# A weight sum taken from VectorE to an adding DMA one block ahead, and DRAM sums spread over a two-layer encoder kernel

## The chip, the cores and the metric

The kernel runs on one NeuronCore of a Trainium2 chip. Its engines run side by side and wait for each other only through semaphores: PE (TensorE, matmuls), DVE (VectorE), ACT (ScalarE), POOL (GpSimd) and SP, which only issues DMAs here. POOL issues DMAs too, and those that add onto their destination are issued by it alone. The metric is the device time of one execution in microseconds.

## The reference, cut to what matters

Two layers work on 512 tokens of width 1024. The first mixes tokens by retention and neighbourhood attention, the second by a state space scan (below: the state space layer). Each is followed by the same channel mixer, and both channel mixers are what the change touches:

```
def conv_geglu_ffn(hn, w_up, conv_w, conv_b, w_down):
    u = depthwise_conv_centered(hn @ w_up, conv_w, conv_b)
    gate, val = jnp.split(u, 2, axis=-1)
    return (jax.nn.gelu(gate, approximate=True) * val) @ w_down
```

w_up is 1024 x 5632 (2816 gate and 2816 value columns), w_down 2816 x 1024. All is float32, and every large product is made of three float32r matmuls: each operand is split into a high part (a cast, on ACT) and a low part (source minus high, on DVE), and high x high, low x high and high x low are summed in PSUM (`mm3`, L125 to L127).

## The kernel before, in words

**The channel mixer's up-projection.** The 2816 columns of each half are 22 tiles of 128, counted by f. Tiles 0 to 5, 20 and 21 are plain. The other 14 are taken in seven Strassen blocks of two tiles each (f = 6, 8, ... 18; blocks 0 to 6 here). A block multiplies a 2 x 2 arrangement of weight quarters (q11, q12, q21, q22, each 128 x 1024 in SBUF) with sums of token halves in seven products (products 0 to 6) instead of eight. A product is 24 matmuls of 128x256. Its stationary operand is a pair of weight parts in one of four places of a buffer named ring. So a place is filled again once the product four before is through, and splitting runs at most about three products ahead of PE.

**What each product needs**, in the function `weights` of `up_strassen`. All loads go through SP.
- Product 0: load q11 into the first-half buffer, split it.
- Product 1: load q12 and q22; DVE adds q12 + q22 into q12 (L469, wst<-wst,wu); DVE adds q11 + q12 into q0 (L469, gain<-wst); POOL issues a DMA that adds a quarter of w_up from DRAM onto q11 (L484); split q12.
- Product 2: split q0. Product 3: load q21, DVE adds it to q0 (L469, gain<-gain), split q0.
- Product 4: split q11, which by then must hold the sum of the DMA above. Products 5 and 6: split q21 and q22.

The three buffers of q11 and q12 (named wst) rotate from block to block; q0 and q21 sit in two others (gain), q22 in wu.

**Around the products.** PSUM results go to tiles G and V by copies (ACT) and adds (DVE, L469). The tails of a block's two tiles (convolution, GELU, product: L531 to L540) are held back and worked off behind products 3 and 5 of the next block. A DVE subtraction of two quarters of H (L329, H<-H, 128x2816), which belongs to the down-projection that follows, becomes ready inside block 3.

**Chores.** The down-projection is a Strassen product as well, and its weight sums are made in DRAM by 32 DMAs per channel mixer (L293, ts): 16 plain copies, then 16 adds, each of a quarter of a quarter (704 KB). They stand in a list. `E.chore()` pops one, ties it to the matmul that was written last, and issues it on POOL. Calls stand in both mixers, behind plain tiles, and in `up_strassen` behind products 1 and 4. In the state space layer they are the letters c in the strings SLOTS, one string per head group, which give the order in which its steps are written: h and i heads and inter-chunk parts, p pairs, n projections of the next group, o output products.

**What sets the order.** Instructions of one engine run in the order in which a scheduler puts them. Split and load of a product have a priority of 60 over their place in the text, and `E.in_turn` keeps them in the order of the products. Across engines only data waits.

Of the kernel before, what the change touches and what calls it, by code (L numbers as in the profile page):

```python
# [8 lines left out]
F32 = mybir.dt.float32  # L9
# [4 lines left out]
ALU = mybir.AluOpType  # L14
# [3 lines left out]
P = 128  # L18
# [385 lines left out]
UP = (6, 8, 10, 12, 14, 16, 18)  # L404
# [41 lines left out]
def up_strassen(E, pool, w_up, f, X, G, V, held):  # L446

    nc, tc = E.nc, E.tc  # L450
    low, high = slice(0, HW), slice(HW, S)

    nth = UP.index(f)
    if f - 2 not in UP:
        E.held = [[E.wst.tile([P, 1024], F32, name="wst") for _ in range(3)],
                  [E.gain.tile([P, D], F32, name="gain") for _ in range(2)]]
    (st12, st11), (st0, st21) = [E.held[0][(2 * nth + j) % 3] for j in range(2)], E.held[1]

    def load(st, s, h):
        E.load = nc.sync.dma_start(st, w_up[s, f + h])  # L460
        return st

    def parts(st, i):
        hi, lo = E.weight(SKEW if i else 0)
        E.split(hi, lo, st)
        E.last = E.pair + (E.load,)
        return hi, lo

    add = lambda o, x, y: nc.vector.tensor_tensor(o, x, y, op=ALU.add)  # L469
    q = {}  # L470

    def weights(i):
        with tc.high_priority(60), E.in_turn():
            if i == 0:
                q[11] = load(st11, 0, 0)
                return parts(q[11], i)
            if i == 1:
                q[12] = load(st12, 1, 0)
                with E.in_turn(E.load):
                    q[22] = load(pool.tile([P, 1024], F32, name="wu", tag=f"e{nth % 2}"), 1, 1)  # L480
                add(q[12], q[12], q[22])
                q[0] = st0
                add(q[0], q[11], q[12])
                nc.gpsimd.dma_start(q[11], w_up[1, f], accum_op=ALU.add, max_dma_last_dim=4096)  # L484
                return parts(q[12], i)
            if i == 2:
                return parts(q[0], i)
            if i == 3:
                q[21] = load(st21, 0, 1)
                add(q[0], q[0], q[21])  # L490
                return parts(q[0], i)
            return parts(q[{4: 11, 5: 21, 6: 22}[i]], i)

    a = E.mm.tile([P, S], F32, name="mm")
    b, d = (E.px.tile([P, S], F32, name="pu", tag="px") for _ in range(2))
    order = ("A11", a), ("S3", b), ("S2", a), ("A22", b), ("R1", a), ("A12", d), ("S4", a)
    for i, (n, bank) in enumerate(order):
        hi, lo = weights(i)
        more = i in (2, 3, 4, 6)
        r = bank.rearrange("p (j c) -> p j c", j=2)  # L500
        for j in range(2):
            for k in range(4):
                c = slice(j * 512 + k * P, j * 512 + k * P + P)
                E.mm3(r[:, j], hi[:, c], lo[:, c], X[n][0][:, k], X[n][1][:, k], not more and j + k == 0, k == 3, more or j > 0)
        if i in (3, 5):
            o = G[:, :, low if i == 3 else high]
            add(o, r, o)
        elif i == 4:
            t = E.tmp.tile([P, 2, HW], F32, name="w5", tag="tmp")
            nc.scalar.copy(t, r)  # L510
            add(V[:, :, low], t, V[:, :, low])
        else:
            nc.scalar.copy({0: G[:, :, high], 1: V[:, :, low], 2: G[:, :, low], 6: V[:, :, high]}[i], r)
        if i in (1, 4):
            E.chore()
        if i in (3, 5) and held:
            held.pop(0)()


def ffn(E, w_up, cw, w_down, ts, g_post_row, done, w1=None):  # L520
# [3 lines left out]
    with ExitStack() as ctx:  # L524
# [44 lines left out]
        for f in range(2, NF):  # L569
            if f in UP or f - 1 in UP:  # L570
                if f in UP:
                    G, V = (cp.tile([P, 2, S], F32, name=n, tag=t) for n, t in
                            ((("G", "k0"), ("V", "k1")) if UP.index(f) % 2 else (("G", "k2"), ("V", "k3"))))
                    up_strassen(E, hp, w_up, f, X, G, V, held)
                    held.extend(partial(tail, f + j, G[:, j], V[:, j], True) for j in range(2))
                    while held and f + 2 not in UP:
                        held.pop(0)()
                continue
            ps = []
            for s in range(2):  # L580
                behind = w1 and f == 2
                with E.in_turn() if f > UP[0] else nullcontext():
                    st = E.wload(w_up[s, f], E.mid if behind and s == 0 else None)
                    w = E.wunit(None, st=st, behind=E.turned[3][1] if behind else None)
                E.last = E.pair + (E.load,)
                ps.append(E.mm.tile([P, S], F32, name="mm"))
                E.proj_fm(ps[-1], w)
            tail(f, *ps)
            E.chore(1 + (f == 2))
            if f < UP[0]:  # L590
                X = next(make)
            if f == NF - 2:
                big = hp.tile([P, 32, HW], R32, name="big")
                for k in range(0, HK, 4):
                    c = slice(k, min(k + 4, HK))
                    E.split(big[:, c], big[:, HK + k:HK + c.stop], H[:, c, HW:])
# [40 lines left out]
def mixer0(E, w0, w_v, w_fm, tabs, dist_d, logit, gn, bias, w_out, g_post_row, done):  # L637
# [286 lines left out]

SLOTS = (
# [4 lines left out]
)  # L930

# [563 lines left out]
```

## Time and profile before

| | |
|---|---|
| median of 3 runs | 1360.77 us (1360.38 to 1362.2) |
| the profiled execution's own time | 1356.96 us |
| its span, first to last instruction | 1355.2 us |
| PE busy | 1325.2 us (98%) |
| DVE busy | 1124.9 us (83%) |
| ACT busy | 841.6 us (62%) |
| POOL busy | 125.5 us (9%) |
| mean granted TensorE clock | 0.998 |

The profiled execution took 3.8 us less than the median of the runs. In the rows below, the columns of the view of stretches are the stretch, its length, then for each engine its busy time and (x) instructions, then the granted clock of PE, the share of the DMA engines and GB/s. A row of the timeline is start, duration, engine, line, operation, out<-in and shape; in brackets, the idle time of the engine before it and what ended that. Matmuls overlap in their records, so PE counts as busy when they follow each other at any pace: the pace is read from the starts.

### The profile page before, as it was taken

What the parts mean: (1) busy time and instruction counts of PE and PEld (TensorE: products, weight loads), DVE (VectorE), ACT (ScalarE), POOL (GpSimd) and SP (SyncE); (2) the same over time, 40 slices, a digit from 0 to 9 for tenths busy, and PEclk for the clock granted to TensorE, in tenths of its full rate; (3) what the DMA queues carried; (4) which work ended last, traced back from release to release, by engine and by line L of the source; (5) the groups of instructions that cost most, each with busy time, mean ns of one, the idle gap of its engine ahead of it and who ended that gap; (6) DMA issues with size and microseconds to landing.
All of it is one profiled execution on the core that took longest, in us unless ns stands there. A gap on an engine that the chain in (4) does not pass through costs nothing.

```text
span 1355.2 us, 20474 instructions
## 1 busy us (share of the span) xinstructions
PE 1325.2 (98%) x7784; PEld 1139.2 (84%) x7784; DVE 1124.9 (83%) x1554; ACT 841.6 (62%) x1353; POOL 125.5 (9%) x144
## 2 busy tenths in 40 slices
PE   7999999999999999999999999999999999999998
PEld 6877777898999988888778788787879899998886
DVE  7368888696799998797878876798789789999886
ACT  5356667453565766664878878477545467666663
POOL 1011111101110000020000110011011111110001
PEclk9999999999999999999999999999999999999999
DMA  8454447348983545564466475285544789684654
GB/s 294 146 208 161 159 135 217 103 123 197 217 206 100 151 143 194 190 210 129 138 181 195 126 247 185 90 250 162 183 133 152 203 197 220 166 225 146 193 183 148
DMA packets 71393, 237.28 MB, mean 175 GB/s; under 512 B 8576, under 2 KB 9344, under 8 KB 70784
## 3 DMA queue, kind: packets, MB, share of 16 engines
q1 hardware_dynamic: 54224, 167.30, 36.8%
q0 software_dynamic: 9184, 53.48, 17.6%
q10 hardware_dynamic: 7888, 15.21, 4.2%
q8 instruction: 61, 1.00, 0.3%
q14 instruction: 36, 0.29, 0.1%
HBM read 228.35 MB, written 51.64 MB: 207 GB/s over the span
## 4 chain that ended last, share of the span: by engine, by line
PE 77%; DVE 10%; ACT 5%; DMA 4%; issue 3%; SPq 1%; POOL 0%; DVEq 0%; POOLq 0%; ACTq 0%
PE mm L125 20%; PE mm L127 20%; PE mm L126 20%; DVE ring L116 3%; PE pu L126 2%; PE pu L125 2%; PE pu L127 2%; DMA pb<-pd 1%; PE pi L1155 1%; PE st L1104 1%; ACT pb L1134 1%; PE py L1175 1%; DVE cv L533 1%; DMA wst<-in_c_fm 1%; PE pt L182 1%
## 5 line engine op out<-in xcount | busy, mean ns | idle before, releaser
L125 PE MATMUL mm<-xh,ring 128*128 128x512 f32 (+1 forms) x880 | 321.0, 365 | 1.3 <-ACT z L1074 0.9
L116 DVE TENSOR_TENSOR ring<-wst,ring 128x1024 fp32r<-128x1024 f32 (+1 forms) x218 | 265.4, 1222 | 67.4 <-ACT ring L115 67.2
L127 PE MATMUL mm<-xl,ring 128*128 128x512 f32 (+2 forms) x880 | 320.0, 364 | 1.1 <-DVE mean L958 0.6
L126 PE MATMUL mm<-xh,ring 128*128 128x512 f32 (+2 forms) x880 | 319.8, 364 | 1.1 <-DVE ring L116 1.1
L115 ACT CAST ring<-wst 128x1024 fp32r<-128x1024 f32 (+1 forms) x218 | 224.4, 1034 | 122.3 <-PE mm L126 64.0
L125 PEld LDWEIGHTS mm<-xh,ring 128*128 128x128 f32 x880 | 165.4, 188 | 29.3 <-issue 2.7
L127 PEld LDWEIGHTS mm<-xl,ring 128*128 128x128 f32 (+1 forms) x880 | 165.1, 188 | 28.1 <-issue 1.1
L126 PEld LDWEIGHTS mm<-xh,ring 128*128 128x128 f32 (+1 forms) x880 | 165.4, 188 | 27.0 <-DVE ring L116 1.7
L125 PE MATMUL mm<-xc,ring 128*128 128x256 f32 x336 | 93.1, 277 | 0.0
L127 PE MATMUL mm<-xc,ring 128*128 128x256 f32 x336 | 93.1, 277 | 0.0
L126 PE MATMUL mm<-xc,ring 128*128 128x256 f32 x336 | 93.1, 277 | 0.0
L1134 ACT ACTIVATE pb<-pb,tok 128x128 f32<-128x128 f32 x256 | 80.7, 394 | 10.0 <-DMA pb<-pd 8.9
L125 PE MATMUL mm<-ring,big 128*128 128x512 f32 x164 | 64.0, 390 | 0.0
L127 PE MATMUL mm<-ring,big 128*128 128x512 f32 x164 | 63.8, 389 | 0.0
L126 PE MATMUL mm<-ring,big 128*128 128x512 f32 x164 | 63.8, 389 | 0.0
L127 PEld LDWEIGHTS mm<-xc,ring 128*128 128x128 f32 x336 | 63.1, 188 | 0.0
L125 PEld LDWEIGHTS mm<-xc,ring 128*128 128x128 f32 x336 | 63.1, 188 | 0.0
L126 PEld LDWEIGHTS mm<-xc,ring 128*128 128x128 f32 x336 | 63.0, 188 | 0.0
L125 PE MATMUL pu<-xh,ring 128*128 128x256 f32 x224 | 62.5, 279 | 0.1
L126 PE MATMUL pu<-xh,ring 128*128 128x256 f32 x224 | 62.3, 278 | 0.1
L127 PE MATMUL pu<-xl,ring 128*128 128x256 f32 x224 | 62.1, 277 | 0.0
L293 POOL DMA_DIRECT2D ts<-in_f_down x48 | 31.0, 652 | 280.3 <-PE mm L127 229.5
(360 smaller groups left out, 3120.8 us busy)
## 6 DMA issues: line engine op xcount, KB each, us to landing
ts<-in_f_down POOLq DMA_DIRECT2D x48, 704.0 KB, 6.3
wst<-in_f_up SPq DMA_DIRECT2D x60, 512.0 KB
wst<-in_c_fm SPq DMA_DIRECT2D x40, 512.0 KB
wst<-ts SPq DMA_DIRECT2D x32, 512.0 KB
pb<-pd ACTq DMA_DIRECT2D x29, 512.0 KB
wst<-in_f_down SPq DMA_DIRECT2D x24, 512.0 KB
ts<-ts POOLq DMA_DIRECT2D x16, 704.0 KB, 7.2
wst<-in_ab_fm SPq DMA_DIRECT2D x20, 512.0 KB
```

The costliest lines, as they stand in the source:

```text
L115: first = self.nc.scalar.copy(hi, src)
L116: second = self.nc.vector.tensor_tensor(lo, src, hi.bitcast(F32), op=ALU.subtract)
L125: mm(out, lh, rh, start=first, stop=False)
L126: mm(out, ll, rh, start=False, stop=False)
L127: self.product = mm(out, lh, rl, start=False, stop=last)
L182: last = nc.tensor.transpose(pt[:, j], xs[:, j * P:(j + 1) * P], self.ident)
L293: out.append(lambda i=i, src=src, j=j, c=c, kw=kw: gp.dma_start(part(ts, i, c), part(src, j, c), **kw))
L533: nc.vector.scalar_tensor_tensor(o[:, :S - 1], ps[:, 1:], w(2), o[:, :S - 1], op0=ALU.mult, op1=ALU.add)
L1104: nc.tensor.matmul(ps, o["bt"][:, c], xs, start=True, stop=True)
L1134: nc.scalar.activation(pb[:, dr, c], pb[:, dr, c], AF.Identity, scale=1.0 - 2 * dr, bias=tok[:, 0, c, dr * H + h:dr * H + h + 1])
L1155: nc.tensor.matmul(pi[:, c - 1 + dr], o["st"][dr, i][:, q * P:(q + 1) * P], o["t"][1][:, c * C:(c + 1) * C], start=True, stop=True)
L1175: E.together([nc.tensor.matmul(py[j * 64:j * 64 + 64, c * C:(c + 1) * C], o["x"][:, c, (2 * q + j) * 64:(2 * q + j + 1) * 64], ms[j][0][:, c],
```

## The change

Of the sums that a block needs, q12 + q22 is no longer made by DVE, except in block 0. In each block but the last, SP loads the next block's q12 into the third of the rotating buffers (`ahead`), and POOL issues a DMA that adds the next block's q22 from DRAM onto it (`onto`). The block's own q22 is still loaded into wu for product 6; that load now stands behind the load of q21. Each load is kept behind the one before it. `E.chore()` behind product 1 goes, so a block issues one chore and not two. Four letters c are added in the strings of head groups 1 and 2 of the state space layer: four chores of the second channel mixer, plain copies, are issued there instead of later.

```diff
--- before.py
+++ after.py
@@ -454,11 +454,19 @@
     if f - 2 not in UP:
         E.held = [[E.wst.tile([P, 1024], F32, name="wst") for _ in range(3)],
                   [E.gain.tile([P, D], F32, name="gain") for _ in range(2)]]
-    (st12, st11), (st0, st21) = [E.held[0][(2 * nth + j) % 3] for j in range(2)], E.held[1]
-
-    def load(st, s, h):
-        E.load = nc.sync.dma_start(st, w_up[s, f + h])
+    first, more_blocks = f - 2 not in UP, f + 2 in UP
+    (st12, st11, ahead), (st0, st21) = [E.held[0][(2 * nth + j) % 3] for j in range(3)], E.held[1]
+
+    def load(st, s, h, f=f):
+        with E.in_turn(E.load):
+            E.load = nc.sync.dma_start(st, w_up[s, f + h])
         return st
+
+    def onto(st, f, h):
+        nc.gpsimd.dma_start(st, w_up[1, f + h], accum_op=ALU.add, max_dma_last_dim=4096)
+
+    def load22():
+        q[22] = load(pool.tile([P, 1024], F32, name="wu", tag=f"e{nth % 2}"), 1, 1)
 
     def parts(st, i):
         hi, lo = E.weight(SKEW if i else 0)
@@ -475,18 +483,24 @@
                 q[11] = load(st11, 0, 0)
                 return parts(q[11], i)
             if i == 1:
-                q[12] = load(st12, 1, 0)
-                with E.in_turn(E.load):
-                    q[22] = load(pool.tile([P, 1024], F32, name="wu", tag=f"e{nth % 2}"), 1, 1)
-                add(q[12], q[12], q[22])
+                q[12] = st12
+                if first:
+                    load(st12, 1, 0)
+                    load22()
+                    add(st12, st12, q[22])
                 q[0] = st0
                 add(q[0], q[11], q[12])
-                nc.gpsimd.dma_start(q[11], w_up[1, f], accum_op=ALU.add, max_dma_last_dim=4096)
+                onto(q[11], f, 0)
                 return parts(q[12], i)
             if i == 2:
+                if more_blocks:
+                    load(ahead, 1, 0, f + 2)
+                    onto(ahead, f + 2, 1)
                 return parts(q[0], i)
             if i == 3:
                 q[21] = load(st21, 0, 1)
+                if not first:
+                    load22()
                 add(q[0], q[0], q[21])
                 return parts(q[0], i)
             return parts(q[{4: 11, 5: 21, 6: 22}[i]], i)
@@ -511,7 +525,7 @@
             add(V[:, :, low], t, V[:, :, low])
         else:
             nc.scalar.copy({0: G[:, :, high], 1: V[:, :, low], 2: G[:, :, low], 6: V[:, :, high]}[i], r)
-        if i in (1, 4):
+        if i == 4:
             E.chore()
         if i in (3, 5) and held:
             held.pop(0)()
@@ -924,8 +938,8 @@
 
 SLOTS = (
     "G s0 s1 t6 t7 s2 i0 h0 t8 t9 S h1 p0 i1 n0 h2 h4 h3 p1 i2 n6 n1 h5 n7 i3 n9 p2 N n3 n4 n2 n5 h6 h7 p3 n8 N",
-    "s0 G R s1 s2 h0 i0 i1 o0 c h1 h2 o1 c p0 h4 h3 p1 h5 i2 n0 c n1 p2 n6 c n3 h6 n7 n2 n9 N i3 n8 h7 p3 n4 n5 N",
-    "G R s0 s1 o0 c h2 o1 c s2 h0 h1 i1 i0 p0 h3 p1 h4 i2 n0 c h5 N n1 n3 c p2 n2 n4 i3 h6 h7 p3 n5 N",
+    "s0 G R s1 s2 h0 i0 i1 o0 c h1 h2 o1 c p0 h4 h3 p1 h5 i2 n0 c n1 p2 n6 c n3 h6 n7 n2 c n9 N i3 n8 c h7 p3 n4 n5 N",
+    "G R s0 s1 o0 c h2 o1 c s2 h0 h1 i1 i0 p0 h3 p1 h4 i2 n0 c h5 N n1 n3 c p2 n2 c n4 c i3 h6 h7 p3 n5 N",
     "G R h0 s0 s1 c t9 h1 t8 c s2 i0 t6 S h2 c t7 p0 i1 S h3 o0 c p1 i2 h4 h5 o1 p2 i3 h6 h7 p3",
 )
 
```

The lines of the changed kernel stand 8 to 14 lower behind this place: L469 is L477 there, L484 is L466, and L532, L533 and L540 are L546, L547 and L554. On PE the order of all matmuls is the same.

DVE in the second channel mixer, from the split for product 6 of block 3 to the split for product 1 of block 4 (ring<-wu: split for product 6; the ring<-wst after it: product 0; the next ring<-wst: product 1; cv: tails). Before:

```order
L116 TENSOR_TENSOR ring<-wu,ring 128x1024
L469 TENSOR_TENSOR G<-pu,G 128x2x256
L329 TENSOR_TENSOR H<-H 128x11x256
L469 TENSOR_TENSOR V<-w_10722,V 128x2x256
L116 TENSOR_TENSOR ring<-wst,ring 128x1024
L469 TENSOR_TENSOR wst<-wst,wu 128x1024
L469 TENSOR_TENSOR G<-pu,G 128x2x256
L532 SCALAR_TENSOR_TENSOR cv_10753<-G,cwt,cv_10753 128x511
L469 TENSOR_TENSOR gain<-wst 128x1024
L533 SCALAR_TENSOR_TENSOR cv_10753<-G,cwt,cv_10753 128x511
L116 TENSOR_TENSOR ring<-wst,ring 128x1024
```

And in the changed kernel:

```order
L329 TENSOR_TENSOR H<-H 128x11x256
L477 TENSOR_TENSOR G<-pu,G 128x2x256
L116 TENSOR_TENSOR ring<-wu,ring 128x1024
L116 TENSOR_TENSOR ring<-wst,ring 128x1024
L477 TENSOR_TENSOR V<-w_10724,V 128x2x256
L477 TENSOR_TENSOR gain<-wst 128x1024
L477 TENSOR_TENSOR G<-pu,G 128x2x256
L116 TENSOR_TENSOR ring<-wst,ring 128x1024
L546 SCALAR_TENSOR_TENSOR cv_10755<-G,cwt,cv_10755 128x511
L546 SCALAR_TENSOR_TENSOR cv_10760<-V,cwn,cv_10760 128x511
L547 SCALAR_TENSOR_TENSOR cv_10755<-G,cwt,cv_10755 128x511
L547 SCALAR_TENSOR_TENSOR cv_10760<-V,cwn,cv_10760 128x511
L116 TENSOR_TENSOR ring<-gain,ring 128x1024
```

The add wst<-wst,wu is gone, H<-H stands ahead of the split for product 6 and no longer behind it, and two convolution steps moved from ahead of the split for product 1 to behind it.

POOL in the second channel mixer, blocks 1 to 4 (wst with the same number is the same buffer). Before, where each wst row is the sum for product 4 of one block:

```order
L484 DMA wst_9899<-in_f1_up 128x1024
L293 DMA ts1_221<-in_f1_down 176x1024 x2
L484 DMA wst_9901<-in_f1_up 128x1024
L293 DMA ts1_221<-in_f1_down 176x1024
L293 DMA ts1_221<-ts1_221 176x1024
L484 DMA wst_9900<-in_f1_up 128x1024
L293 DMA ts1_221<-ts1_221 176x1024 x2
L484 DMA wst_9899<-in_f1_up 128x1024
```

And in the changed kernel, where of each two wst rows the first is the sum for product 4 of a block, and the second, once that buffer is read and loaded again, the q12 + q22 of the block two further on:

```order
L466 DMA wst_9903<-in_f1_up 128x1024 x2
L293 DMA ts1_221<-ts1_221 176x1024
L466 DMA wst_9905<-in_f1_up 128x1024 x2
L293 DMA ts1_221<-ts1_221 176x1024
L466 DMA wst_9904<-in_f1_up 128x1024 x2
L293 DMA ts1_221<-ts1_221 176x1024
L466 DMA wst_9903<-in_f1_up 128x1024 x2
```

Three DMAs a block stand there as before, one more of them an add onto SBUF and one fewer a chore, and each sum for product 4 now has a chore and an add of a whole quarter just ahead of it.

## The prediction

> **What bounds the kernel now.** I read the page's first part, then the waits of PE, then the stretches of the Strassen blocks, and last the timeline of DVE and ACT where PE waits.
>
> ```profile
> span 1355.2 us, 20474 instructions
> PE 1325.2 (98%) x7784; PEld 1139.2 (84%) x7784; DVE 1124.9 (83%) x1554; ACT 841.6 (62%) x1353; POOL 125.5 (9%) x144
> ...
> PE pt L182 <- DVE xs L173: 9.9, 4, 7.3
> PE pu L126 <- DVE ring L116: 4.2, 2, 2.2
> ```
>
> PE is the bound, and its order of matmuls doesn't change. So the change can only win what PE loses around the Strassen blocks. The second wait is there: PE waits for a low part of a split, twice, 4.2 us. What it costs is seen in the stretches of one block each (first channel mixer blocks 3 to 6, second blocks 0 to 6 without 3):
>
> ```profile
> 398.21:417.84 19.63, 19.57 (x170) 19.37 (x169) 19.49 (x21) 12.10 (x17) 0.28 (x1) 1.00 0.52 146
> 417.84:442.30 24.46, 22.10 (x170) 21.55 (x169) 23.15 (x28) 15.20 (x20) 0.87 (x1) 0.93 0.37 109
> 442.30:462.20 19.90, 19.90 (x170) 19.90 (x169) 19.90 (x24) 13.59 (x18) 0.86 (x1) 1.00 0.51 159
> 462.20:481.74 19.54, 19.54 (x170) 19.54 (x169) 19.54 (x25) 14.88 (x20) 0.89 (x1) 1.00 0.53 162
> ...
> 1083.42:1102.62 19.20, 19.20 (x169) 19.18 (x168) 14.36 (x15) 10.90 (x13) 3.52 (x4) 1.00 0.82 180
> 1102.62:1121.83 19.21, 19.21 (x171) 19.21 (x169) 16.79 (x20) 13.78 (x18) 2.68 (x3) 1.00 0.88 210
> 1121.83:1141.03 19.20, 19.20 (x171) 19.20 (x169) 19.03 (x23) 13.06 (x17) 2.68 (x3) 1.00 0.90 215
> ...
> 1160.22:1182.68 22.46, 20.37 (x170) 19.97 (x169) 22.46 (x27) 15.28 (x20) 2.68 (x3) 1.00 0.73 187
> 1182.68:1202.59 19.91, 19.89 (x171) 19.70 (x170) 19.91 (x24) 13.59 (x18) 2.68 (x3) 1.00 0.90 227
> 1202.59:1221.81 19.22, 19.22 (x171) 19.22 (x169) 19.22 (x25) 14.56 (x20) 1.82 (x2) 1.00 0.72 184
> ```
>
> An undisturbed block takes 19.2 us, 2.72 a product and 2.88 for product 0. DVE's share of it grows from 14.36 to all of it (22.46 of 22.46). Above 19.2 the first mixer pays 0.43 + 5.26 + 0.70 + 0.34 = 6.7 us, the second 3.26 + 0.71 + 0.02 = 4.0. **10.7 us is the most that can be won here.** Block 4 holds most of it:
>
> ```profile
> 421.40:423.60 2.20, 0.01 (x1) 0.00 (x0) 2.20 (x4) 2.17 (x4) 0.87 (x1) 1.00 0.00 0
> 424.50:427.90 3.40, 3.40 (x18) 3.40 (x17) 3.40 (x5) 0.00 (x0) 0.00 (x0) 0.50 0.96 235
> 1163.30:1165.40 2.10, 0.08 (x2) 0.00 (x1) 2.10 (x4) 2.07 (x4) 0.89 (x1) 1.00 0.00 0
> ```
>
> PE stands for 2.20 and some 2.1 us, and in the first mixer the granted clock then is 0.50 for 3.40 us: 1.7 us more. The rest is pace: block 5 takes 0.7 us more with next to no wait, because matmuls that were once held up follow each other more slowly for a while. (The Trainium skill, "TensorE: Matmul & The Clock Gate", section "What's actually happening", lets the clock fall to half after an idle window of about 3.4 us. The trace differs: 2.20 us were enough once. By the rule 1.7 of the 10.7 us would not be there to win; by the row they are.)
>
> **Why PE waits**, second mixer, end of block 3 and start of block 4 (DVE, and one row of ACT):
>
> ```profile
> 1155.20 3.08 DVE L329 TENSOR_TENSOR H<-H 128x2816 f32<-128x2816 f32 x1
> 1158.20 0.69 DVE L469 TENSOR_TENSOR V<-w,V 128x512 f32<-128x512 f32 x1
> 1158.80 1.22 DVE L116 TENSOR_TENSOR ring<-wst,ring 128x1024 fp32r<-128x1024 f32 x1
> 1159.93 1.22 DVE L469 TENSOR_TENSOR wst<-wst,wu 128x1024 f32<-128x1024 f32 x1
> 1161.07 0.68 DVE L469 TENSOR_TENSOR G<-pu,G 128x512 f32<-128x512 f32 x1
> 1161.67 0.74 DVE L532 SCALAR_TENSOR_TENSOR cv<-G,cwt,cv 128x511 f32<-128x511 f32 x1
> 1162.33 1.22 DVE L469 TENSOR_TENSOR gain<-wst 128x1024 f32<-128x1024 f32 x1
> ...
> 1164.13 1.22 DVE L116 TENSOR_TENSOR ring<-wst,ring 128x1024 fp32r<-128x1024 f32 x1
> ...
> 1161.24 1.05 ACT L115 CAST ring<-wst 128x1024 fp32r<-128x1024 f32 x1 [4.25 <-DVE wst L469]
> ```
>
> DVE never rests. From start to start a 128x1024 operation costs 1.13 us, a 512-wide one 0.60, a convolution step 0.66, H<-H 3.00. The cast for product 1 itself waits 4.25 us for the add that the change removes. A full block asks of DVE ten 1024-wide operations, three 512-wide adds and two tails of four steps and a product: 11.3 + 1.8 + 6.5 = 19.6 us against PE's 19.2. That is why the lead melts, and the 3.00 us of H<-H finish it.
>
> **The change, part by part.** *The add by DVE.* It goes in six blocks of seven, in both mixers:
>
> ```profile
> L469 DVE TENSOR_TENSOR wst<-wst,wu 128x1024 f32<-128x1024 f32 x14 | 17.1, 1219 | 0.0
> ```
>
> 12 x 1.13 = 13.6 us of DVE. A block then asks 18.5 us, under PE's 19.2, so the lead no longer melts from block to block. To see whether H<-H still hits PE, I run down DVE's new order in the prices above. The lead is the time from the end of a low part to its product. At product 0 of block 3 I take the 5.65 us that block 2's has (low part 1114.95 + 1.23, product at 1121.83), the ring being full:
>
> ```profile
> 1109.25 1.23 DVE L116 TENSOR_TENSOR ring<-wst,ring 128x1024 fp32r<-128x1024 f32 x1 [1.48 <-ACT ring L115]
> ...
> 1114.95 1.23 DVE L116 TENSOR_TENSOR ring<-wst,ring 128x1024 fp32r<-128x1024 f32 x1 [0.40 <-ACT ring L115]
> ...
> 1121.83 0.28 PE L125 MATMUL mm<-xh,ring 128*128 128x256 f32 x1
> ```
>
> Up to product 1 of block 4, DVE has 2.9 + 3.7 + 4.2 + 1.8 + 2.5 + 5.3 + 1.1 + 3.5 = 25.0 us to do, PE eight products, 22.1: a lead of 2.8. Before, it was 1160.22 + 2.88 - (1164.13 + 1.22) = -2.2. The same count over the old order, from block 2's product 0, has 48.2 us of work against 41.3 of PE and gives -1.2, so it flatters by 0.5 a block. Two products on, 3.8 and 4.2 us of work face 5.4 of PE: 0.2. From this 0.5 comes off for that error, and up to 0.9 because product 4's split may wait for its DMA. So product 3 of block 4 is late by 0.3 to 1.2 us. Then PE again pays some 0.7 us in pace, as block 5 shows. I leave 1.0 to 2.8 us per mixer, centre 1.8, and the 0.50 clock is not met, since it came behind 2.20 us of standing and not behind 2.1.
>
> Sum: 10.7 - 2 x 1.8 = **7.1 us saved**; bounds 10.7 (nothing left) and 5.1 (2.8 left in each).
>
> *The DMAs on POOL.* Twelve more adds of 512 KB from DRAM onto SBUF; the trace has 14 of this kind:
>
> ```profile
> L484 POOL DMA_DIRECT2D wst<-in_f_up x14: 860/888/908, 331.2 to 1203.5; - x14
> ...
> DMA to landing us min/median/max: 5.2/7.0/9.6
> ```
>
> A block's q12 sum is issued once product 4's split of the block two back is read and the buffer loaded again, over 20 us ahead of its split. Even 9.6 us hides. Tighter is the sum for product 4, which now has a chore and such an add before it:
>
> ```profile
> 1097.84 0.86 POOL L293 DMA_DIRECT2D ts<-in_f_down  x1 [7.36 <-PE mm L127]
> 1099.98 0.88 POOL L484 DMA_DIRECT2D wst<-in_f_up x1 [1.27 <-DVE V L469]
> 1108.16 1.05 ACT L115 CAST ring<-wst 128x1024 fp32r<-128x1024 f32 x1 [1.44 <-DMA wst<-in_f_up]
> ...
> 1113.66 0.28 PE L125 MATMUL mm<-xc,ring 128*128 128x256 f32 x1
> ```
>
> 2.1 us behind a chore it took 8.2 us, the cast waited for it, and the low part ended 1110.48: 3.2 us of lead at 1113.66. The added DMA goes out about 6 us before it (the split for product 4, 3 us for the load, then POOL) and should be through: cost 0. From both sides: a gain of nothing, since a chore stood there before too; a loss of 3.0 us a DMA still in flight (8.2 - 5.2) would use up the 3.2 us and no more.
>
> At this place a rule speaks against the change. The Trainium skill ("SBUF — State Buffer", section "SBUF: two separate sides", the "DVE blocks DMA" trap) says that descriptors of POOL's DMAs can't be written while DVE holds a port that both share in its two-port modes. The trace disagrees for these operations:
>
> ```profile
> L484 POOL DMA_DIRECT2D wst<-in_f_up x1: 891/891/891, 463.1 to 463.1; - x1
> ...
> DMA to landing us min/median/max: 5.2/5.2/5.2
> ```
>
> At 463.1 DVE is busy all of the stretch (19.54 of 19.54), and the landing is the fastest of all. By the rule the new sums would land only when DVE pauses, which is rival 2 with its 1369 us; by the row they cost nothing and the sum stays 7.1.
>
> *Loads, chores.* SP issues as many loads as before; q22's moves behind q21's but is needed three products later. A second chore per block goes: no engine waited for those. The four copies in the state space layer stand in POOL's queue ahead of `sq` adds:
>
> ```profile
> 808.79 0.53 POOL L293 DMA_DIRECT2D ts<-in_f_down  x1
> 841.68 1.28 POOL L1187 TENSOR_TENSOR sq<-sq 128x512 f32<-128x512 f32 x1 [32.37 <-ACT sq L1181]
> ```
>
> POOL idles 32.37 us there, and the copies wait for matmuls that end before the `sq`. Cost 0; if their traffic holds up weights or rows, about 1 us, hence 0 to 1. The last two chores now fall on tiles 20 and 21, three products of the down-projection before they are read.
>
> **Rivals.**
> 1. *The stall only moves.* H<-H now stands ahead of the split for product 6 of block 3 and still takes 3.00 us. If the lead at block 3 is 3 and not 5.65 us (a late DMA left 3.2), product 6 and products 2 and 3 of block 4 each come late, and half of the 10.7 stays, with one clock drop of 1.7: saved 2 to 4, 1357 to 1359, 1358 in the middle. Against it: 3.4 us less DVE work by then.
> 2. *The sum for product 4 becomes the bound* (slower). If the added DMA and the chore both are in flight before it, it takes 5.2 + 2 x 3.0 to 5.2 + 2 x 4.4 (9.6 - 5.2) = 11.2 to 14.0 us from issue. From 3.2 us of lead at 8.2, it decides from 11.4 on: 0 to 2.6 us in each of blocks 1 to 6. The middle, 1.3 x 12 = 15.6, less 7.1: 8.5 slower, 1369. For it: DMA engines at 0.90 in blocks with three POOL DMAs. Against: those blocks had no late product 4.
> 3. *It doesn't show*: other DVE waits, or the state space layer, take back 5 of 7 us: 1359 to 1363.
>
> **How the numbers follow.** The sum stands against the profiled execution: 1356.96 - 7.1 = 1349.9. That one is 3.8 us under the median of the runs; I leave this difference as it is: 1360.77 - 7.1 = **1353.7 us**, own range 1350 to 1356.5. About 0.2% (2.7 us) is what a measurement can tell from no change, so faster is below 1358.0 and slower above 1363.5. Chances: forecast 0.62, rival 1 0.17, rival 2 0.09, rival 3 0.12. Faster: 0.62, half of rival 1 and a little of rival 3's edge, together 0.73; slower 0.09; same 0.18. Range for 8 in 10: the forecast's own, rival 1 and the start of rival 3: 1349.5 to 1359.5.
>
> **What would show it.** Right: no PE wait of 2 us for ring in either block 4, granted clock at 1.00 through both mixers, blocks 5 at 19.2 to 19.5, DVE with idle time in blocks 1 to 3, and a small wait at product 3 of block 4. Rival 1: a wait at product 6 of block 3, or one over 1.5 us at product 3. Rival 2: casts of wst that wait for DMA wst in every block, landings over 11 us. Wrong altogether: block lengths as before with the add gone, so that DVE's sum was not what held PE; or PE waits in the state space layer at the new copies.

## The result, and the profile after

The changed kernel takes 1378.22 us (median of 4 runs, 1377.01 to 1381.16), the kernel before 1360.58: ratio 1.014, 95% interval 1.0116 to 1.0164, so 1.4% slower. The prediction was 1353.7, in a range from 1349.5 to 1359.5: the wrong side of no change.

The profiled execution took 1377.01 us. The page's first lines, and the longest waits of PE, of the changed kernel:

```profile
span 1375.2 us, 20491 instructions
PE 1331.0 (97%) x7784; PEld 1143.0 (83%) x7784; DVE 1112.4 (81%) x1542; ACT 839.9 (61%) x1353; POOL 134.6 (10%) x156
...
PE pu L125 <- ACT V L527: 16.4, 12, 2.0
PE pt L182 <- DVE xs L173: 9.7, 4, 7.3
PE mm L125 <- DVE xf L1082: 4.7, 3, 3.0
```

DVE did become lighter (1124.9 to 1112.4), and the wait for `ring` of product 1 (4.2 us, two times) is gone. In its place stands a new wait, 12 times: once in each of blocks 1 to 6 of both channel mixers, always ahead of product 3, for ACT's copy V<-pu that empties the PSUM bank of product 1. A third row, 4.7 us for xf, belongs to the state space layer.

The view of stretches by stage shows where the span grew. Before (first mixer's blocks, a stretch of 50 matmuls in the state space layer, second mixer's blocks), then after:

```profile
340.61:481.85 141.24, 138.82 (x1178) 138.06 (x1177) 131.38 (x150) 92.59 (x121) 11.54 (x13) 0.99 0.63 166
848.16:859.42 11.26, 10.45 (x52) 8.48 (x51) 5.96 (x8) 7.90 (x17) 0.00 (x0) 1.00 0.26 87
1083.43:1221.81 138.38, 136.28 (x1178) 135.67 (x1176) 130.82 (x149) 92.55 (x121) 17.87 (x20) 1.00 0.83 202
```

```profile
340.39:488.01 147.62, 138.92 (x1178) 137.52 (x1177) 126.23 (x144) 92.33 (x121) 16.16 (x18) 1.00 0.72 177
854.52:870.02 15.50, 12.31 (x52) 9.52 (x50) 5.95 (x8) 9.84 (x23) 0.00 (x0) 0.89 0.26 101
1093.33:1241.80 148.47, 140.61 (x1178) 139.38 (x1177) 126.37 (x144) 92.28 (x122) 16.99 (x19) 0.99 0.73 177
```

The same matmuls take 6.4 us more in the first mixer and 9.9 in the second (the last stretch ends 0.2 us behind the mark used for that difference), 4.2 in the one short stretch of the state space layer; everything else together is 0.5 shorter, which makes the 20.0 us between the two spans. In the short stretch the granted clock is 0.89: 3.41 us of it run at half clock, so 1.7 of the 4.2 us come from the clock. Between the medians lie 17.6 us; the first profile of the kernel before was an execution 3.6 us under its median.

The new wait, followed back in block 2 of the first mixer, in the timeline of POOL, ACT and PE and the view of DMA landings:

```profile
374.00 0.86 POOL L466 DMA_DIRECT2D wst<-in_f_up  x1 [17.36 <-DMA wst<-in_f_up]
375.50 0.91 POOL L293 DMA_DIRECT2D ts<-ts  x1 [0.64 <-PE mm L127]
376.39 0.95 POOL L466 DMA_DIRECT2D wst<-in_f_up  x1
...
L466 POOL DMA_DIRECT2D wst<-in_f_up x1: 952/952/952, 376.4 to 376.4; - x1
DMA to landing us min/median/max: 11.9/11.9/11.9
...
388.33 1.05 ACT L115 CAST ring<-wst 128x1024 fp32r<-128x1024 f32 x1 [3.33 <-DMA wst<-in_f_up]
389.82 0.57 ACT L527 COPY V<-pu 128x512 f32<-128x512 f32 x1
...
390.44 0.39 PE L125 MATMUL pu<-xh,ring 128*128 128x256 f32 x1 [1.38 <-ACT V L527]
```

Three DMAs go out within 2.4 us: the q12 sum for a later block, the chore, and last the one that is needed first, the sum for product 4. It lands after 11.9 us. ACT's cast for product 4 waits 3.33 us for it, the copy of product 1 is queued behind that cast (with a step of a tail between them), and PE can't start product 3 because its bank isn't empty. In the twelve blocks PE stands 0.8 to 2.1 us longer between two matmuls there than elsewhere, goes on at a slower pace, and once, in block 1 of the second mixer, has half the clock for 3.4 us.

The two blocks 4 carry the same name in that row of waits, but not the same cause. Here is the one of the second mixer, ACT, DVE and PE:

```profile
1184.64 1.05 ACT L115 CAST ring<-gain 128x1024 fp32r<-128x1024 f32 x1 [2.42 <-DVE gain L477]
1185.60 1.04 ACT L115 CAST ring<-wst 128x1024 fp32r<-128x1024 f32 x1
1185.85 1.22 DVE L116 TENSOR_TENSOR ring<-gain,ring 128x1024 fp32r<-128x1024 f32 x1
1187.18 0.39 PE L125 MATMUL pu<-xh,ring 128*128 128x256 f32 x1 [1.07 <-ACT V L527]
```

The cast for product 4 waits for no DMA: its sum took 6.7 us and had landed. ACT waited for DVE, and product 3's own low part ends only at 1185.85 + 1.22 = 1187.07. In the first mixer the cast waits 0.35 us for the sum, and 2.43 for DVE stand ahead of it. These two waits, 2.3 of the 16.4 us, are mostly DVE's; the other ten are the late sum's.

The place in the state space layer, POOL, ACT and PE of the changed kernel, then ACT of the kernel before:

```profile
843.29 0.49 POOL L293 DMA_DIRECT2D ts<-in_f_down  x1 [14.88 <-PE mm L127]
847.28 1.52 ACTq L1137 DMA_DIRECT2D pb<-pd  x1
856.84 2.79 ACT L1148 ACTIVATE pb<-pb,tok 128x128 f32<-128x128 f32 x9 [5.38 <-DMA pb<-pd]
859.54 0.76 ACT L1079 ACTIVATE xf<-mm,cwt 128x512 f32<-128x512 f32 x1
860.82 0.47 PE L125 MATMUL mm<-ring,yh 128*128 128x512 f32 x1 [2.97 <-DVE xf L1082]
```

```profile
840.91 0.37 ACTq L1123 DMA_DIRECT2D pb<-pd  x1
846.26 2.75 ACT L1134 ACTIVATE pb<-pb,tok 128x128 f32<-128x128 f32 x9 [1.18 <-DMA pb<-pd]
```

One of the four added chores goes out 4.0 us ahead of a row load (pb<-pd) and lands 2.6 us behind the start of that load. ACT waits 5.38 us for rows where it waited 1.18, the evacuation of xf stands behind that, and PE waits 2.97 us. It is the same shape as in the mixers: a DMA that is late stops ACT's queue, and a PSUM bank behind it stays full.

### The profile page after: what moved, and what is told of

It reads as the page before. It is cut to its first block, busy times and chain, and to the rows that moved or that the text cites. A ratio compares the mean times of both kernels' runs of the same rounds, so it can differ in the third digit from the quotient of the medians.

```text
span 1375.2 us, 20491 instructions
## 1 busy us (share of the span) xinstructions
PE 1331.0 (97%) x7784; PEld 1143.0 (83%) x7784; DVE 1112.4 (81%) x1542; ACT 839.9 (61%) x1353; POOL 134.6 (10%) x156
## 5 line engine op out<-in xcount | busy, mean ns | idle before, releaser
L1148 ACT ACTIVATE pb<-pb,tok 128x128 f32<-128x128 f32 x256 | 80.8, 392 | 15.7 <-DMA pb<-pd 14.3
L125 PE MATMUL pu<-xh,ring 128*128 128x256 f32 x224 | 64.2, 287 | 16.4 <-ACT V L527 16.4
L115 ACT CAST ring<-gain 128x1024 fp32r<-128x1024 f32 x42 | 44.1, 1049 | 23.9 <-DVE gain L477 21.4
```

Of the source, the lines that this page charges most:

```text
L115: first = self.nc.scalar.copy(hi, src)
L125: mm(out, lh, rh, start=first, stop=False)
L1148: nc.scalar.activation(pb[:, dr, c], pb[:, dr, c], AF.Identity, scale=1.0 - 2 * dr, bias=tok[:, 0, c, dr * H + h:dr * H + h + 1])
```

## The experiments

**Where does PE hang, at the bank or at the split?** Theory A: the order on ACT makes the price, since the copy of product 1 stands behind a cast that waits. Theory B: the sum itself is too late, wherever the copy stands. The edit ties the cast for product 4 behind the copy:

```diff
-        with tc.high_priority(60), E.in_turn():
+        with tc.high_priority(60), E.in_turn(*E.last, *([E.copied] if i == 4 else [])):
```

> The changed kernel, with the copy of product 1 (V<-pu) put ahead of the cast for product 4 in ACT's order, and nothing else. Theory A (the late sum stops ACT's queue: the cast for product 4 waits for the adding DMA, the copy that empties product 1's bank stands behind it, and PE waits for the bank at product 3): the sum still lands 11 to 12 us after its issue, the twelve waits of PE for V<-pu (16.4 us) are gone, since product 4's low part ends 0.4 to 1.2 us ahead of where an undisturbed PE would want it; blocks of 19.2 to 19.8 us, 1353 to 1361 us in all. Theory B (product 4's own split is what holds PE): the waits only move from product 3 to product 4, time within 4 us of 1378.

Measured: 1376.39 us, ratio to before 1.0143 (1.0107 to 1.0178). The copies of product 1 are no longer waited for, but the waits go on (longest waits of PE, then block 3 of the first mixer):

```profile
PE mm L125 <- ACT G L527: 10.8, 9, 2.4
...
L466 POOL DMA_DIRECT2D wst<-in_f_up x1: 1237/1237/1237, 397.7 to 397.7; - x1
DMA to landing us min/median/max: 14.1/14.1/14.1
...
411.82 1.05 ACT L115 CAST ring<-wst 128x1024 fp32r<-128x1024 f32 x1 [3.34 <-DMA wst<-in_f_up]
413.72 0.58 ACT L527 COPY G<-mm 128x512 f32<-128x512 f32 x1
414.34 0.55 PE L125 MATMUL mm<-xc,ring 128*128 128x256 f32 x1 [2.24 <-ACT G L527]
```

PE now waits one product later, at product 4, for the copy of product 2, and the low part of product 4's split ends only 0.2 us earlier. Block 1 of the first mixer, with a landing of 12.2 us, ran without a wait, but in blocks 2 and 3 the sums landed after 13 and 14 us, since PE was no longer held back and all that POOL issues came closer together. Theory B holds in the main. The order on ACT decides at which product the wait shows, and has a part of the price: the mixers are 12.6 us longer than before in e1 and 16.3 in the changed kernel (3.4 and 1.7 of that is half clock).

**Why is the sum late?** Either because of the two DMAs ahead of it in POOL's queue (A1) or for some other reason, such as the traffic of loads (C). One run takes the chore from ahead of it, one the q12 sum, one both.

```diff
-        if i == 4:
+        if i == 1:          # e2; e5: if i == 2
             E.chore()
...
-                    onto(ahead, f + 2, 1)          # e3 and e5:
+                    E.together([onto(ahead, f + 2, 1)], [E.product])
```

> The changed kernel, with the one chore of a block behind product 1 and no longer behind product 4, so that only the next block's q12 sum is in flight just ahead of the sum for product 4. Theory A1 (two DMAs in flight ahead of it make that sum late): it lands 8 to 9 us after issue, the waits at product 3 are gone, 1353 to 1361 us. Theory C (the sum is slow for another reason, as the traffic of loads or 26 adding DMAs in place of 14): landing still over 10 us, most of the 16.4 us of waits stay, 1370 or more.

> The changed kernel, with the next block's q12 sum tied to the end of product 1 of the running block, so that only a chore is in flight just ahead of the sum for product 4. Theory A1: it lands 8 to 10 us after issue, as before the change; waits at product 3 gone, q12 sum ready 5 us or more ahead of its cast, 1353 to 1361 us. Theory C: landing over 10 us, 1370 or more.

> The changed kernel with both moves: the next block's q12 sum tied to the end of product 1 of the running block, the chore behind product 2. If POOL's DMAs are worked off one behind the other, the sum for product 4 now meets an empty queue and lands in 5 to 6 us in every block; no PE wait at product 3 or 4 for it; both channel mixers together 7 to 9 us shorter than in the kernel before, the state space layer still some 5 us longer: 1355 to 1358 us. If the sums are slow by something else than their place in the queue: landings above 8 us as in the two single moves, and no gain over those (1358 and 1363.5).

| | time, us | ratio to before (95%) | landing of the sum for product 4, blocks 1 to 6, first mixer | mixers against the first profile of before |
|---|---|---|---|---|
| changed kernel | 1378.22 | 1.014 (1.0116 to 1.0164) | 8.0 to 11.9 | +6.4, +9.9 |
| e2, chore moved | 1357.98 | 0.9992 (0.9972 to 1.0012) | 5.3 to 10.5 | -3.8, -1.6 |
| e3, q12 sum moved | 1363.55 | 1.0027 (1.0009 to 1.0046) | 5.3 to 10.3 | -2.8, +1.3 |
| e5, both moved | 1356.65 | 0.9971 (0.9953 to 0.9988) | 5.5 to 9.2 | -4.2, -1.5 |

As what makes most of the price theory C is out: with the same 26 adding DMAs and the same loads, only their order changed, the two mixers together are 21.9 us shorter in e5 than in the changed kernel (16.3 to -5.7; 1.7 of it is the half clock in block 1). Moving the chore alone already brings 21.6. Not every number came as expected: e2's landings spread wider than 8 to 9 us, and e3's 1363.55 lies above the 1353 to 1361 that were forecast, with a sum of 10.9 us in block 2 of the second mixer (that block 1.4 us longer) and 3.0 us in the state space layer's short stretch.

The order isn't all of it. For block 6 no q12 sum goes ahead, only a chore, 2.3 us ahead and onto an empty queue. Its landing in the changed kernel, first mixer:

```profile
L466 POOL DMA_DIRECT2D wst<-in_f_up x1: 896/896/896, 463.6 to 463.6; - x1
DMA to landing us min/median/max: 10.9/10.9/10.9
```

The chore took 9.4 us there and the sum 10.9 (10.5 in the second mixer), where the kernel before, with a chore 2.1 to 2.3 us ahead, had sums of 8.2 to 8.9; PE waited in both blocks 6. SP issued three loads between 457.5 and 458.4, just ahead of the two; that their traffic made the difference was not tested.

For e5 too my number for the landings was wrong. Here is the landing in block 2 of the first mixer, then in block 4 (view of DMA landings):

```profile
L466 POOL DMA_DIRECT2D wst<-in_f_up x1: 914/914/914, 375.9 to 375.9; - x1
DMA to landing us min/median/max: 8.5/8.5/8.5
...
L466 POOL DMA_DIRECT2D wst<-in_f_up x1: 896/896/896, 418.2 to 418.2; - x1
DMA to landing us min/median/max: 5.7/5.7/5.7
```

I expected 5 to 6 us in every block. The chore, issued 6.4 us ahead, stood itself behind the q12 sum and was still under way. Where the chore was through, as in block 4, the sum took 5.7; in block 6, where it was all but through (it landed 0.4 us later), 8.2. What the sum still costs in e2 and e3 comes with landings around 10 us (block 2 of e2: 10.5, and that block is 1.3 us longer; block 2 of e3: 10.3, 0.7 longer). With those of up to 9.2 us in e5 some casts for product 4 still wait, up to 1.74 us, but PE doesn't. What waits of PE for V<-pu are left in e5 stand in block 4 of both mixers, at product 3:

```profile
427.33 0.38 PE L125 MATMUL pu<-xh,ring 128*128 128x256 f32 x1 [0.73 <-ACT V L527]
1171.40 0.39 PE L125 MATMUL pu<-xh,ring 128*128 128x256 f32 x1 [0.56 <-ACT V L527]
...
426.01 1.21 DVE L116 TENSOR_TENSOR ring<-gain,ring 128x1024 fp32r<-128x1024 f32 x1
```

The first mixer's low part for product 3 is ready only at 426.01 + 1.21 = 427.22: DVE again, at the place and with the size (0.3 to 1.2 us) that the prediction's count gave.

**What is it worth to free DVE?** The kernel before without the add q12 + q22; the sum is left out, so q12 enters its products alone, and no DMA takes its place.

```diff
                 q[12] = load(st12, 1, 0)
...
-                add(q[12], q[12], q[22])
```

> The kernel before without the add q12 + q22: the sum is left out, q12 goes alone into its products, and no DMA takes its place. It measures what freeing DVE is worth by itself. By the prediction's count (18.5 us of DVE work in a block of 19.2): PE's waits in both blocks 4 and the 0.50 clock are gone, 5 to 9 us less, 1352 to 1356 us. If DVE's add is not what held PE: 1359 to 1362.

Measured: 1355.56 us, 0.9957 (0.9943 to 0.9971), 5 us less. Block 4 of both mixers, view of stretches:

```profile
419.12:439.06 19.94, 19.91 (x171) 19.72 (x169) 19.90 (x24) 13.88 (x19) 1.62 (x2) 1.00 0.48 136
1160.42:1180.97 20.55, 19.89 (x170) 19.70 (x169) 20.52 (x25) 14.48 (x19) 3.57 (x4) 1.00 0.84 201
```

Before they took 24.46 and 22.46 (23.06 and 22.42 in another profile of the same kernel, e9 below). So DVE's add was what held PE there.

**What is left of it?** By the prediction the 3.0 us of H<-H. In e6 and e8 both moves are kept, and two of the chores added in the state space layer, those of head group 2, go to product 5 of the last two blocks (`if i == 2 or i == 5 and nth > 4`); e8 also makes H<-H in three pieces:

```diff
-            tt(A21, A11, A21, op=ALU.subtract)
+            for c in (slice(0, 4), slice(4, 8), slice(8, HK)):
+                tt(A21[:, c], A11[:, c], A21[:, c], op=ALU.subtract)
```

> As with both moves, and besides the two chores added in head group 2 of the state space layer go to product 5 of the last two Strassen blocks (the two in head group 1 stay). If these two alone held the row loads up: no PE wait of over 1.5 us for xf there, the layer within 1 us of the kernel before, and 3 to 5 us less than with both moves alone: 1350 to 1354 us. If the two of head group 1 matter as much: half of that, 1353 to 1356.

> As e6 (both moves, two chores moved), and H<-H of 128x2816 split in three pieces of 1024, 1024 and 768, which may stand in blocks where DVE idles. If the 3.0 us of this one operation are what is left in blocks 3 to 5 (3 to 4 us in both mixers after the single move of the chore): blocks 3 to 5 at 19.2 to 19.4, 1 to 3 us less than e6, 1348 to 1352. If what is left comes from the sums or the loads: equal to e6.

e6 takes 1357.27 us (0.9971, 0.9958 to 0.9983), no less than e5 and above both ranges that were expected of it. e8 takes 1353.62 (0.9942, 0.9921 to 0.9964). Block 4 of both mixers in e8:

```profile
417.24:437.05 19.81, 19.81 (x170) 19.80 (x169) 19.77 (x25) 14.68 (x20) 2.68 (x3) 1.00 0.81 206
1158.83:1178.64 19.81, 19.81 (x170) 19.80 (x169) 19.77 (x25) 14.68 (x20) 2.68 (x3) 1.00 0.82 201
```

Against the first profile of before the mixers are 4.4 and 2.3 us shorter in e6, 6.2 and 3.4 in e8: 9.6 of the 10.7 us that were there to win. H<-H was most of what was left: blocks 5 and 6 are at 19.2 us in e8, block 4 keeps 0.6 in each mixer, and at 1353.62 it stays above the expected 1348 to 1352. That e6 gained nothing on e5 spoke against my choice of the guilty chores, which the next runs settle.

**What do the chores in the state space layer cost?** In e4 the kernel before gets the four chores alone: the order on POOL is the only one that differs. e10 is e8 with none of the four (they go to product 5 of the last four blocks), e11 is e8 again beside it, and e9 the kernel before once more, for its profile.

> The kernel before, with the four further chores in the state space layer alone. If these copies by themselves delay the row loads (pb<-pd) for which ACT waits, and with them PE: PE waits of 1.5 and 3 us for xf in head group 2, 3.5 to 5 us more in the layer, 1364 to 1366 us. If the delay in that layer came only from the phase in which the first channel mixer left the kernel: 1360 to 1361 us.

> The kernel before once more, for its profile. The state space layer was 2.8 us longer than in the first profile of the kernel before even in the kernel without the add, whose order of chores there is the old one. If the layer's length changes by some us from execution to execution: this profile has it 1 to 5 us longer than the first too. If the first profile is what this kernel always does there: within 0.5 us of it.

> As e8 (both moves, H<-H in three pieces), with the state space layer's chores as in the kernel before: none of the four is added there, they go to product 5 of the last four Strassen blocks. If the added chores cost 3 to 5 us in that layer: 1349 to 1351. If the layer varies by itself and the chores cost under 1 us: within 1 us of e8's 1353.6.

> The kernel of e8 once more, on the same chip as e10, to compare the two: 1352 to 1355 us.

e4: 1362.71 us, 1.0026 (1.0006 to 1.0046), between its two expected ranges. e9: 1358.49. e10: 1350.95, 0.9929 (0.991 to 0.9948). e11: 1353.23, 0.9951 (0.9933 to 0.9969). The stretch of 50 matmuls shown above, first in e4, then in e8, then in e10:

```profile
850.48:864.64 14.16, 10.68 (x52) 8.40 (x50) 5.93 (x8) 9.78 (x23) 0.00 (x0) 1.00 0.28 105
```

```profile
843.48:858.83 15.35, 10.72 (x51) 8.39 (x50) 5.93 (x8) 9.78 (x23) 0.00 (x0) 1.00 0.26 97
```

```profile
844.24:855.40 11.16, 10.45 (x52) 8.47 (x50) 5.97 (x8) 7.81 (x17) 0.00 (x0) 1.00 0.24 89
```

It is 2.6 to 4.9 us longer in all nine profiles with the added chores of head group 1 (the changed kernel, e1 to e6, e8, e11), and within 0.2 us of the first profile of before in the three that don't (e7, e9, e10). e6 and e8 show that those of head group 2, which I had moved, are not the ones. So two chores of head group 1 cost this stretch some 3 to 5 us; in five of the nine (the changed kernel, e1, e2, e5, e11) 1.7 of it is half clock behind the wait. Not all of it reaches the end. The part of the layer ahead of this stretch is 0.8 us longer in the changed kernel, up to 4.4 in others, and 3.2 in e9, which is the kernel before: it varies from execution to execution. In e6, e7 and e9, the three with more than 3 us, 1.7 of that is again half clock. In the medians of e10 and e11 2.3 us are left.

## Why the prediction was wrong, point by point

- **The sum for product 4** is the step that failed: "should be through: cost 0". I counted on some 6 us between the added DMA and it, and took 3.0 us for each DMA still in flight. Measured: 5.4 us in block 1 of the first mixer, 2.4 to 3.9 in all others that have such a DMA ahead (blocks 1 to 5) but the two blocks 4 (6.9 and 7.6), because the buffer that the added DMA fills is free only once product 4's split is through, and that split was late itself. And the two others in flight cost together up to 6.7 us of 11.9 (11.9 less the 5.2 of a sum alone), in the second mixer up to 7.5 of 12.7. In place of nothing it cost 21.9 us (the mixers of the changed kernel against e5). What made the sums of block 6 late, with only a chore ahead, is open in part.
- **Rival 2** named the mechanism, with a chance of 0.09 and 8.5 us slower; it came out 17.6 slower. Its lead of 3.2 us was read at the low part of product 4, where it decides from 11.4 us of landing on. In the changed kernel ACT's copy of product 1 stands behind the cast, and PE needs the bank a product earlier, so it decided from some 10 us on (10.5 in e2 cost 1.3 us, 9.2 in e5 nothing). I had not asked what is queued behind the waiting cast on ACT, though the prediction quoted that cast with its wait. What stood "against" it didn't carry over: in such a block of the kernel before the three DMAs went out over 11.4 us (1128.00 to 1139.36), here within 2.4 in block 2 of the first mixer, since the late product 4 made the next added DMA late.
- **By DVE's load** the forecast was right. The block's sum of 18.5 us against 19.2, and with it the end of the stall in block 4, came as said: block 4 of the first mixer took 20.96 us in the changed kernel, where the wait at product 3 was mostly DVE's, and 19.9 in e7. The term of 7.1 us, bounded by 5.1 and 10.7, measured 4.7 in e7, 5.7 in e5 and 6.8 in e6. Against e9's profile in place of the first one each of these is 1.1 us less. What e6 leaves over, 2.3 and 1.7 us, lies in the 1.0 to 2.8 a mixer that were left for H<-H, though the 2.8 are more than the parts named there (1.2 of lateness and 0.7 of pace) add up to. e5 shows the wait at product 3 of block 4 as counted, and e8 that most of it was H<-H.
- **The rule that was set aside**: the Trainium skill ("SBUF — State Buffer", section "SBUF: two separate sides", the "DVE blocks DMA" trap) had spoken for a slower kernel. The sums were late, but not for that reason: in e5 the sum of 418.2 lands in 5.7 us while DVE is busy for the whole of its block (first row), and while the late ones of the changed kernel were under way DVE idled, for 0.8 to 4.0 us with the ten that held PE, as in block 2 of the first mixer (second row, from issue to landing: 9.85 of 11.92 us busy). No row shows whether DVE's operations here are of the kind that the rule means.

```profile
418.12:438.74 20.62, 19.89 (x170) 19.70 (x169) 20.62 (x25) 14.30 (x20) 3.57 (x4) 1.00 0.83 195
...
376.39:388.31 11.92, 11.92 (x104) 11.92 (x104) 9.85 (x13) 6.95 (x10) 0.96 (x2) 1.00 0.94 190
```

- **The copies in the state space layer** were put at 0 to 1 us, with the `sq` adds behind them on POOL in view. It was the row loads of ACT that came late behind them: 4.2 us in the changed kernel's profile (1.7 of it half clock), 2.9 in e4's.
- **The rest of the numbers**: that PE's order and the loads of SP cost nothing held. That the 10.7 us are all there to win did not quite: 1.7 us of them is the stretch at half clock, which e9, the same kernel, didn't have (block 4 of the first mixer 23.06 us at clock 1.00, where the first profile has 24.46 at 0.93).

## What to carry to other kernels

Where work goes from a busy engine to DMAs of an engine that issues others, put all of them in the order of issue and add up their landing times one behind the other: the one that is needed first must not go last, and its place can be worth more (here 21.9 us) than the work saved (5 to 7). For each wait on a DMA ask what stands behind the waiting instruction on its engine, down to the PSUM bank that PE needs next. The version that keeps the change, issues the early sums after the urgent one, moves the chores away from the row loads and cuts H<-H in three (e10) takes 1350.95 us, 0.7% less than the kernel before.

## What the runs showed of the hardware that was not expected

**POOL's DMAs are worked off largely one behind the other.** Of the three of block 2 the first took 5.9 us, the second 9.9, the third 11.9 from its own issue: 14.3 us from the first issue to the last landing, against 5.2 for a sum and some 6.3 for a chore with the queue empty, which would be 16.7 for the three strictly in turn. (The Trainium skill, "DMA: Bandwidth & Descriptors", section "Queues, rings and completion order", says of the DMAs that SP and ACT issue that each DMA engine takes their descriptors in the order of the ring, while a later DMA may still complete first. These three of POOL landed in the order of issue.) The same DMAs in another order, e5, gave 5.4 to 9.2 for the sum.

**The half clock doesn't follow the length of the wait alone.** In the changed kernel PE stood 2.1 us at 410.2 and kept full clock, and 2.0 us at 1120.9, after which it had half for 3.4 us:

```profile
410.20:412.30 2.10, 0.13 (x3) 0.01 (x1) 1.03 (x1) 2.10 (x4) 0.00 (x0) 1.00 0.00 0
1120.90:1122.90 2.00, 0.10 (x1) 0.00 (x0) 0.48 (x1) 1.56 (x3) 0.00 (x0) 1.00 0.00 0
1124.40:1127.80 3.40, 3.40 (x19) 3.40 (x18) 2.53 (x3) 1.48 (x2) 0.04 (x1) 0.50 0.88 242
```

In e9 the wait of 2.2 us that had brought half clock in the first profile of the same kernel did not. The traces show what goes with it. Within a profile the starts of half clock lie whole multiples of 3.413 us apart (here 1124.40 - 861.58 = 262.82 = 77 x 3.413), and each stretch but the last of a profile is 3.41 us long. Cut into windows on that grid, the thirteen profiles have thirteen such stretches between 60 and 1330 us. Each follows a window in which PE stood for 1.91 us or more; the windows without half clock behind them have 1.80 or less. The two waits above, seen in their windows:

```profile
411.02:414.43 3.41, 2.13 (x18) 2.13 (x19) 3.12 (x4) 3.41 (x6) 0.00 (x0) 1.00 0.25 61
1120.99:1124.40 3.41, 1.49 (x14) 1.48 (x14) 1.77 (x2) 3.06 (x5) 0.00 (x0) 1.00 0.00 0
```

A border at 411.02 divides the first wait, so that 1.28 us fall in this window and 0.70 in the one ahead; the second lies whole in one, with 1.92. In the first profile of the kernel before 2.20 us lay whole in a window, in e9 only 1.67. That the grid decides is read from the traces; no run was made to test it.
